# Output projection of an encoder trunk: four of eight feature tiles in the attention chain and four with the norm, the tokens in halves

## The chip, the cores and the metric

The kernel runs on one core of one Trainium2 chip. The metric is the device time of one execution in microseconds (us); a kernel's time is the median of its runs. TensorE (PE) multiplies, VectorE (DVE) and ScalarE (ACT) split, add and evict, GpSimd (POOL) adds a part of the norm's sums, and SyncE (SP) issues most of the loads.

## What is computed

Two requests, 512 and 256 tokens wide, go through the same two layers. Here only what lies around the output projection matters:

```python
def encoder_trunk(x, ...):
    for layer in range(DEPTH):            # DEPTH = 2, D_MODEL = 1024, D_FF = 4096
        if layer % 2 == 0:
            ...                           # windowed and grouped-query attention
            x = x + jnp.concatenate([a_out, b_out], axis=-1) @ w_out_e[j]
        else:
            ...                           # differential attention, norm of each head
            x = x + o.reshape(B, T, DIFF_WIDTH) @ w_out_o[j]
        h = rmsnorm(x, ln_mlp[layer])
        x = x + jnp.square(jax.nn.relu(h @ w_up[layer])) @ w_down[layer]
    return rmsnorm(x, ln_f)
```

## The kernel before

All 768 tokens stand side by side, features on the 128 partitions. `x` has eight tiles of 128 x 768, and so has `o`, the output of attention. A product is made in three matmuls, since every fp32 operand is split into a rounded part (`whi`, `oh`, `xh`) and the rest (`wlo`, `ol`, `xl`): hi by hi, lo by hi, hi by lo. ACT makes the rounded part and DVE the rest.

**Attention and its chain.** An attention unit is one head (or pair of heads) for 128 queries: scores on PE (`gs`, `ns`, `ds`), a softmax on DVE and ACT, a transposition on PE (`npt`, `dpt`), the product with the values (`npv`, `dpv`), and in the odd layer a norm of the head on ACT, DVE and POOL and one more transposition (`otp`). `attention` sets 48 units in a row. While a unit's softmax runs, PE works on the `Chain`: the input projections and, as its last member, `out_proj` (L762 to L774). The chain is pulled a step at a time, and `ramp` (L634, L759) says by a list of marks how many steps stand beside each group of six units. Between the scores of a unit and its transposition stand the chain's steps of that unit and the value product of the unit before.

**The output projection** is in two parts. `out_proj` multiplies the first six tiles of `o` in the chain: for each of the eight feature tiles `m` 18 pairs of matmuls, one of 512 columns (`opa`) and one of 256 (`opb`) with the same weights, a step being the three pairs of one `k`: 48 steps in a layer. `out_proj_norm` (L776 on) follows when the chain is drained. It multiplies the last two tiles of `o` for one half of the tokens (384 columns) at a time, as `opc` (`product`, L788): six matmuls for each `m` and half. After each, DVE adds the result onto `x[m]`, ACT squares it, and POOL or DVE adds the square onto `acc`.

**The norm.** When half 0 is through, `woven` (L817) sets three pieces of half 1 (`m` 0 to 2, 3 to 5, 6 and 7) around the norm of half 0: after the first piece the sums over the partitions (`ss`, L172) and the power (`rt`, on POOL), after the second the spreading of `rt` over the partitions (`pb`, L195) and its copy `R` (L199), and then `split_half`: for each `k` a normed `xn` (L803), its `xh` (L806) and its `xl` (L807). The first matmuls of the up projection (`upc`, L883) take `xh` and `xl` of half 0, and stand right behind the third piece.

**What sets the order.** The order on each engine is made ahead of the run by a scheduler that goes by the order of the code and an estimate of what is ready. In the trace each engine runs its instructions in that order, so one that waits holds up all that is queued behind it. Buffers come from pools: four pairs `whi`/`wlo` of weights, nine `xo` tiles that hold `o` and `x` alike, three PSUM banks "mm" and five "at".

Of the kernel before, what the change touches and what calls it, by code (L numbers as in the profile page):

```python
# [12 lines left out]
F32 = mybir.dt.float32  # L13
F32R = mybir.dt.float32r
AF = mybir.ActivationFunctionType
# [31 lines left out]
def kernel(ctx: ExitStack, tc: tile.TileContext, a: dict, y: bass.AP):  # L47
# [23 lines left out]
    def ps_tile(tag, name):  # L71
        return psum.tile([P, 512], F32, tag=tag, name=name, bufs=BANKS[tag])
# [141 lines left out]
    def proj_feat(lhs, xs, ks, pa, pb, cols=SEGS, nk=None, pin=False):  # L214


        nk = len(ks) if nk is None else nk
        for k in ks:
            xh, xl = xs[k]
            for i, (part, mv) in enumerate(((0, xh), (0, xl), (1, xh))):  # L220
                for ps, (s, e) in ((pa, cols[0]), (pb, cols[1])):
                    if ps is not None:
                        mm = nc.tensor.matmul(ps[:, : e - s], lhs(k, part), mv[:, s:e],  # L223
                                              start=(k == 0 and i == 0), stop=(k == nk - 1 and i == 2))
                        if pin and k == 0 and i == 0:
                            tc.keep_in_program_order(mm)
            yield

    def run(gen):
        for _ in gen:  # L230
# [93 lines left out]
    def even_attention():  # L324
# [306 lines left out]
                       lambda: out_proj("w_out_e", o, lambda m: a["xT"][:, m, :], x)])  # L631
        units = [G(gqa_unit, j, t) for j in range(4) for t in range(TT)]
        units += [G(na_unit, p, t) for p in range(4) for t in range(TT)]
        attention(units, chain, ramp((52, 72, 88, 104, 120, 140, 172, 196, 232)))  # L634
        chain.drain()
        return o, x, es

# [1 line left out]
    def odd_attention(xs, nm, sg, spill):  # L639
# [116 lines left out]
            order += [G(proj_v, h // 2)] * (h % 2 == 0) + [G(proj_qk, h)]  # L756
        chain = Chain(order + [lambda: out_proj("w_out_o", o, lambda m: spill[:, m, :], x)])
        units = [G(diff_unit, h, t) for h in range(8) for t in range(TT)]
        attention(units, chain, ramp((56, 92, 128, 164, 200, 236, 272, 306, 336)))  # L759
        chain.drain()  # L760
        return o, x, es


    def out_proj(src, o, xsrc, x):

        os_ = [split(o[k], "o") for k in range(6)]
        for m in range(KD):
            hi, lo = wtile(src, 6 * P)
            pa, pb = ps_tile("mm", "opa"), ps_tile("mm", "opb")
            yield from proj_feat(lambda k, prt: (hi, lo)[prt][:, k * P : (k + 1) * P], os_, range(6), pa, pb)  # L770
            x[m] = xo_tile("x1")
            nc.sync.dma_start(x[m], xsrc(m))
            xm = x[m]
            evac_halves(pa, pb, lambda ps, s: nc.vector.tensor_tensor(out=xm[:, s], in0=ps, in1=xm[:, s], op=ALU.add))  # L774

    def out_proj_norm(src, o, x, g, mp):  # L776


        os_ = [split(o[k], "o") for k in (6, 7)]
        ws = [wtile(src, 1024) for _ in range(2)]  # L780
        up_ws = [[wtile("w_up", 1024) for _ in range(2)]]
        hs = [htiles(mp) for _ in range(GF)]
        acc = cpool.tile([P, NT], F32, tag="acc", name="acc", bufs=1)
# [1 line left out]
        xs = [None] * KD  # L785
        norms = [Norm(lambda: mp.tile([P, NH], F32, tag="st", name="sq", bufs=3), half, acc) for half in EVEN]

        def product(i, m):  # L788

            sl = slice(*EVEN[i])  # L790
            ps = ps_tile(("mm", "at")[m % 2], "opc")[:, :NH]
            hi, lo = ws[m // 4]
            for k in range(2):
                for j, (part, mv) in enumerate(((0, os_[k][0]), (0, os_[k][1]), (1, os_[k][0]))):
                    c = ((m % 4) * 2 + k) * P
                    last = nc.tensor.matmul(ps, (hi, lo)[part][:, c : c + P], mv[:, sl],
                                            start=(k == 0 and j == 0), stop=(k == 1 and j == 2))
            nc.vector.tensor_tensor(out=x[m][:, sl], in0=ps, in1=x[m][:, sl], op=ALU.add)
            norms[i].add(x[m], KD - 1)
            return last  # L800

        def normed(k, out, s):
# [26 lines left out]
                        split_half(i)  # L829
                last = nm.last  # L830

        products = lambda i, ms: lambda: [product(i, m) for m in ms][-1]
        products(0, range(KD))()
        woven(0, [products(1, ms) for ms in (range(3), range(3, 6), range(6, 8))])

        hold = [cpool.tile([P, NT], F32, tag="acc", name="t4", bufs=1), xo_tile("t4")]
# [414 lines left out]
def _layout(i):  # L1251
# [24 lines left out]

    def out_layout(w):
        w = w.reshape(8, P, KD, P)
        p0 = w[:6].transpose(2, 1, 0, 3).reshape(-1)
        p1 = w[6:].reshape(2, P, 2, 4, P).transpose(2, 1, 3, 0, 4).reshape(-1)  # L1280
        return np.concatenate([p0, p1])

    wx = i["w_out_e"][0]
    d["w_out_e"] = out_layout(np.concatenate([wx[hcols(512, heads)], wx[:512]], 0))
# [59 lines left out]
```

## Time and profile before

| | us |
|---|---|
| median of 3 runs | 1769.04 (1768.12 to 1770.06) |
| the profiled execution | 1770.32 |
| its span, first to last instruction | 1768.6 |
| PE busy in the span | 1731.0 (98%) |
| DVE, ACT, POOL busy | 1253.4, 924.8, 223.8 |
| mean granted TensorE clock | 0.996 of full speed |

The times inside the kernel are counted from the start of the span. A busy PE is not a PE at its peak, since matmuls overlap and their ends are modelled: where two matmuls follow each other, what the second costs is the distance between the two starts. A gap in brackets in the timeline is idle time of the engine just before the row, and behind the arrow stands what ended it.

### The profile page before, as it was taken

To read this page: it belongs to the slowest core of one execution; us is meant where nothing else is said; L and a number is where in the kernel's file an instruction comes from. 1 tells how busy PE (TensorE), PEld (TensorE's weight loads), DVE (VectorE), ACT (ScalarE), POOL (GpSimd) and SP (SyncE) were. 2 spreads that over 40 slices of the span, in tenths; PEclk is the share of its full clock that TensorE was granted. 3 is DMA by queue.
4 is the path that set the end of the run, shared out by engine and by line. 5 is a ranking of instruction groups with operands and counts; after the bars stand their busy time and mean duration, and the time that the engine had idled before them with its cause. 6 is when DMAs were issued, how large, how long until landed. Compare 5 with 4: busy or idle time off the path is not lost.

```text
span 1768.6 us, 28926 instructions
## 1 busy us (share of the span) xinstructions
PE 1731.0 (98%) x11146; PEld 1648.6 (93%) x11146; DVE 1253.4 (71%) x2446; ACT 924.8 (52%) x1933; POOL 223.8 (13%) x302
## 2 busy tenths in 40 slices
PE   7999999999999999999999999999899999999998
PEld 7878888899999999999999999988899999999997
DVE  7878646569566669877566767776696666687775
ACT  6765544345566664552435555554455666645434
POOL 3421000020000000110221212220200000001101
PEclk9999999999999999999999999999999999999999
DMA  5111123312466556653311101122123656466622
GB/s 179 49 34 38 65 82 98 122 36 66 140 183 183 170 182 218 196 128 113 133 49 49 49 25 43 48 61 95 43 66 100 187 183 188 144 245 177 160 83 72
DMA packets 55786, 198.24 MB, mean 112 GB/s; under 512 B 6496, under 2 KB 9312, under 8 KB 50528
## 3 DMA queue, kind: packets, MB, share of 16 engines
q1 hardware_dynamic: 42112, 148.39, 26.0%
q0 software_dynamic: 8064, 14.68, 5.3%
q10 hardware_dynamic: 5472, 33.32, 5.2%
q8 instruction: 88, 1.44, 0.3%
q14 instruction: 50, 0.41, 0.1%
HBM read 158.62 MB, written 36.96 MB: 111 GB/s over the span
## 4 chain that ended last, share of the span: by engine, by line
PE 84%; DVE 7%; DMA 4%; ACT 2%; issue 2%; POOL 1%; POOLq 0%; DVEq 0%; ACTq 0%; SPq 0%
PE upx L949 12%; PE dnx L949 9%; PE dqk L209 8%; PE upz L949 6%; PE dnz L949 4%; PE dvp L209 4%; PE upc L883 4%; PE opa L223 4%; DMA hf<-h 3%; PE upy L949 3%; PE dnb L223 3%; PE dna L223 3%; PE npa L223 2%; PE ds L291 2%; PE dny L949 2%; PE dpv L734 2%
## 5 line engine op out<-in xcount | busy, mean ns | idle before, releaser
L91 DVE TENSOR_TENSOR wlo<-wraw,whi 128x1024 fp32r<-128x1024 f32 (+4 forms) x252 | 235.4, 938 | 144.1 <-ACT whi L90 143.7
L90 ACT ACTIVATE whi<-wraw 128x1024 fp32r<-128x1024 f32 (+4 forms) x248 | 203.4, 825 | 163.4 <-PE dnx L949 79.6
L209 PE MATMUL dqk<-whi,xh 128*128 128x256 f32 x384 | 115.6, 301 | 0.0
L209 PE MATMUL dqk<-whi,xl 128*128 128x256 f32 x384 | 108.6, 283 | 0.0
L209 PE MATMUL dqk<-wlo,xh 128*128 128x256 f32 x384 | 108.4, 282 | 0.0
L719 ACT ACTIVATE de<-ds,m 128x512 f32<-128x512 f32 (+1 forms) x96 | 58.3, 613 | 79.9 <-DVE m L717 79.7
L97 POOL DMA_DIRECT2D wlo<-in_w_up_dram x28 | 24.8, 886 | 452.5 <-DVE hf L969 273.7
L209 PEld LDWEIGHTS dqk<-whi,xh 128*128 128x128 f32 x384 | 73.1, 190 | 8.5 <-issue 7.7
L949 PE MATMUL upx<-xh,whi 128*128 128x384 f32 x224 | 74.8, 334 | 0.0
L949 PE MATMUL upx<-xl,whi 128*128 128x384 f32 x224 | 74.8, 334 | 0.0
L949 PE MATMUL upx<-xh,wlo 128*128 128x384 f32 x224 | 74.8, 334 | 0.0
L949 PE MATMUL upx<-Th,whi 128*128 128x384 f32 x224 | 74.8, 334 | 0.0
L949 PE MATMUL upx<-Tl,whi 128*128 128x384 f32 x224 | 74.8, 334 | 0.0
L949 PE MATMUL upx<-Th,wlo 128*128 128x384 f32 x224 | 74.8, 334 | 0.0
L209 PEld LDWEIGHTS dqk<-wlo,xh 128*128 128x128 f32 x384 | 73.3, 191 | 0.0
L209 PEld LDWEIGHTS dqk<-whi,xl 128*128 128x128 f32 x384 | 73.1, 190 | 0.0
L95 ACT ACTIVATE whi<-wraw 128x512 fp32r<-128x512 f32 x56 | 35.2, 629 | 70.2 <-PE upy L949 36.6
L1063 DVE TENSOR_TENSOR x<-x,dnx 128x384 f32<-128x384 f32 x96 | 52.8, 550 | 22.8 <-PE dnx L949 22.7
L687 DVE SCALAR_TENSOR_TENSOR t<-dqk,rt,ropeO 128x128 f32<-128x128 f32 x192 | 57.6, 343 | 8.1 <-PE dqk L209 8.1
L158 POOL TENSOR_TENSOR acc<-acc,sq 128x384 f32<-128x384 f32 (+2 forms) x24 | 31.2, 1302 | 249.8 <-ACT sq L153 249.0
L90 ACT ACTIVATE whi<-ws 128x1024 fp32r<-128x1024 f32 (+2 forms) x52 | 51.8, 997 | 21.1 <-PE dnz L949 15.1
L97 POOL DMA_DIRECT2D wlo<-in_w_down_dram x28 | 24.6, 879 | 289.9 <-ACT wlo L96 148.4
(347 smaller groups left out, 6092.6 us busy)
## 6 DMA issues: line engine op xcount, KB each, us to landing
wraw<-in_w_up_dram SPq DMA_DIRECT2D x64, 512.0 KB, 3.6
h<-hf ACTq DMA_DIRECT2D x20, 1344.0 KB, 5.2
hf<-h SPq DMA_DIRECT2D x20, 1344.0 KB, 7.2
wraw<-in_w_down_dram SPq DMA_DIRECT2D x52, 512.0 KB, 3.5
wraw<-in_w_in_o_dram SPq DMA_DIRECT2D x24, 512.0 KB, 3.6
wraw<-in_w_in_e_dram SPq DMA_DIRECT2D x16, 512.0 KB, 3.7
wlo<-in_w_up_dram POOLq DMA_DIRECT2D x28, 256.0 KB, 6.1
wlo<-in_w_down_dram POOLq DMA_DIRECT2D x28, 256.0 KB, 4.9
```

Of the source, the lines that this page charges most:

```text
L90: nc.scalar.activation(hi, raw, AF.Copy)
L91: nc.vector.tensor_tensor(out=lo, in0=raw, in1=hi.bitcast(F32), op=ALU.subtract)
L97: nc.gpsimd.dma_start(lo, src, accum_op=ALU.add)
L209: nc.tensor.matmul(ps[:, :256], st[:, tk], col(k, part, 0, 256), start=(k == 0 and i == 0), stop=(k == KD - 1 and i == 2))
L223: mm = nc.tensor.matmul(ps[:, : e - s], lhs(k, part), mv[:, s:e], start=(k == 0 and i == 0), stop=(k == nk - 1 and i == 2))
L291: nc.tensor.matmul(out[h], q(a_, hp, qs), k(b_, hp, ks), start=i == 0, stop=i == 2)
L687: nc.vector.scalar_tensor_tensor(out=tt[:, c].rearrange("p (a d) -> p a d", d=32), in0=ps[:, c].rearrange("p (a d) -> p a d", d=32), scalar=r,
L719: nc.scalar.activation(e, s, AF.Exp, bias=m, scale=1.0, accum_out=l2[:, c : c + 1])
L734: nc.tensor.matmul(pv, pt[:, i * P : (i + 1) * P], v[:, k0 // P + i, vc], start=(i == 0), stop=(i == nk - 1))
L883: last = nc.tensor.matmul(ps, lhs(f0 + f, k, part), mv[:, s:e], start=(n == 0 and j == 0), stop=(n == KD - 1 and j == 2))
L949: mm = nc.tensor.matmul(ps, w[part][:, c], mv, start=(start and kk == 0 and j == 0), stop=(stop and kk == len(form) - 1 and j == 2), skip_ ...
L1063: nc.vector.tensor_tensor(out=xm[:, c], in0=xm[:, c], in1=ps, op=op)
```

## The change

The output projection is cut anew. In the chain, `out_proj` takes the first four tiles of `o` instead of six, and for each `m` it goes through the two halves of the tokens in turn (`proj_half`), 12 matmuls of 384 columns each, all named `opa`, in two steps: 32 steps in a layer instead of 48. `out_proj_norm` takes the other four tiles, 12 matmuls instead of six for each `m` and half. The rounded parts and rests of its last two tiles are made in the pool of the MLP (`Th`, `Tl`) instead of `oh` and `ol`. The first four `m` of half 0 run through `k` 0 and 1 for all four before `k` 2 and 3. The weights of the norm's part need four pairs of buffers instead of two, so that those of the up projection, which are asked for right behind, wait for the output projection's to be done with. The marks of `ramp` follow the shorter chain.

```diff
+    def proj_half(lhs, xs, ps, cols):
+        s, e = cols
+        for k in range(len(xs)):
+            xh, xl = xs[k]
+            for i, (part, mv) in enumerate(((0, xh), (0, xl), (1, xh))):
+                nc.tensor.matmul(ps[:, : e - s], lhs(k, part), mv[:, s:e], ...)
+            if k % 2 == 1:
+                yield
-        attention(units, chain, ramp((52, 72, 88, 104, 120, 140, 172, 196, 232)))
+        attention(units, chain, ramp((52, 72, 88, 104, 120, 142, 172, 193, 216)))
-        attention(units, chain, ramp((56, 92, 128, 164, 200, 236, 272, 306, 336)))
+        attention(units, chain, ramp((56, 91, 128, 163, 200, 236, 270, 297, 320)))
     def out_proj(src, o, xsrc, x):
-        os_ = [split(o[k], "o") for k in range(6)]
+        os_ = [split(o[k], "o") for k in range(KH)]
         for m in range(KD):
-            hi, lo = wtile(src, 6 * P)
-            pa, pb = ps_tile("mm", "opa"), ps_tile("mm", "opb")
-            yield from proj_feat(..., os_, range(6), pa, pb)
+            if m % 2 == 0:
+                w = wtile(src, 1024)
             x[m] = xo_tile("x1")
             nc.sync.dma_start(x[m], xsrc(m))
-            evac_halves(pa, pb, lambda ps, s: nc.vector.tensor_tensor(out=xm[:, s], in0=ps, ...))
+            for s, e in EVEN:
+                ps = ps_tile("mm", "opa")
+                yield from proj_half(..., os_, ps, (s, e))
+                nc.vector.tensor_tensor(out=x[m][:, s:e], in0=ps[:, :NH], in1=x[m][:, s:e], op=ALU.add)
     def out_proj_norm(src, o, x, g, mp):
-        os_ = [split(o[k], "o") for k in (6, 7)]
-        ws = [wtile(src, 1024) for _ in range(2)]
+        os_ = [split(o[k], "o") for k in (4, 5)]
+        for k in (6, 7):
+            os_.append([mp.tile([P, NT], F32R, tag=t, name=t, bufs=6) for t in ("Th", "Tl")])
+            nc.scalar.activation(os_[-1][0], o[k], AF.Copy)
+            nc.vector.tensor_tensor(out=os_[-1][1], in0=o[k], in1=os_[-1][0].bitcast(F32), ...)
+        ws = [wtile(src, 1024) for _ in range(4)]
-        def product(i, m):
-            ps = ps_tile(("mm", "at")[m % 2], "opc")[:, :NH]
-            for k in range(2):
+        def product(i, ms):
+            ps = {m: ps_tile(("mm", "at")[m % 2], "opc")[:, :NH] for m in ms}
+            for ks in ((0, 1), (2, 3)):
+                for m in ms:
+                    for k in ks:
...
-        products(0, range(KD))()
+        product(0, range(4))
+        products(0, range(4, KD))()
         woven(0, [products(1, ms) for ms in (range(3), range(3, 6), range(6, 8))])
```

The layout of the two output weights on the host follows.

The first place is the queue of DVE in the norm stage of the even layer, around the copy `R`. Of the names, `x_...<-opc` is the addition of one `m` of half 1, `wlo<-wraw,whi` the rest of a weight tile of the up projection, `acc<-acc,sq` the norm's sum. Before:

```order
L798 TENSOR_TENSOR x_3997<-opc,x_3997 128x384
L91 TENSOR_TENSOR wlo<-wraw,whi 128x1024
L798 TENSOR_TENSOR x_4081<-opc,x_4081 128x384
L798 TENSOR_TENSOR x_4165<-opc,x_4165 128x384
L199 COPY R<-pb 128x384
L158 TENSOR_TENSOR acc<-acc,sq 128x384
L803 SCALAR_TENSOR_TENSOR xn<-x_3717,gains,R 128x384
L803 SCALAR_TENSOR_TENSOR xn<-x_4081,gains,R 128x384
L803 SCALAR_TENSOR_TENSOR xn<-x_3831,gains,R 128x384
L798 TENSOR_TENSOR x_4249<-opc,x_4249 128x384
L807 TENSOR_TENSOR xl<-xn,xh 128x384 x3
```

The same stretch now:

```order
L817 TENSOR_TENSOR x_3840<-opc,x_3840 128x384
L91 TENSOR_TENSOR wlo<-wraw,whi 128x1024
L817 TENSOR_TENSOR x_3912<-opc,x_3912 128x384
L817 TENSOR_TENSOR x_4005<-opc,x_4005 128x384
L199 COPY R<-pb 128x384
L91 TENSOR_TENSOR wlo<-wraw,whi 128x1024
L158 TENSOR_TENSOR acc<-acc,sq 128x384
L822 SCALAR_TENSOR_TENSOR xn<-x_3635,gains,R 128x384
L822 SCALAR_TENSOR_TENSOR xn<-x_3912,gains,R 128x384
L822 SCALAR_TENSOR_TENSOR xn<-x_3701,gains,R 128x384
L826 TENSOR_TENSOR xl<-xn,xh 128x384 x3
```

A weight tile's rest has come between `R` and the first `xn`, and the addition of `m` 6 has left its place ahead of the first `xl`. The other engine's side of this stretch is short to tell: between `pb` and the first `upc` PE has 24 matmuls `opc` where it had 12, and as many more in each of the pieces ahead.

The second place is the queue of PE at the end of the odd layer's attention, where the last unit's value product `dpv` and the last `otp` stand. Before:

```order
L312 MATMUL otp<-ident,o_tok 128x128
L796 MATMUL opc<-oh,whi 128x384
L796 MATMUL opc<-ol,whi 128x384
L796 MATMUL opc<-oh,wlo 128x384
L796 MATMUL opc<-oh,whi 128x384
L796 MATMUL opc<-ol,whi 128x384
L734 MATMUL dpv<-dv_12401,dpt 128x128 x2
L796 MATMUL opc<-oh,wlo 128x384
L796 MATMUL opc<-oh,whi 128x384
L796 MATMUL opc<-ol,whi 128x384
L796 MATMUL opc<-oh,wlo 128x384
L312 MATMUL otp<-ident,o_tok 128x128
```

The same stretch now:

```order
L323 MATMUL otp<-ident,o_tok 128x128
L814 MATMUL opc<-oh,whi 128x384
L814 MATMUL opc<-ol,whi 128x384
L814 MATMUL opc<-oh,wlo 128x384
L814 MATMUL opc<-oh,whi 128x384
L814 MATMUL opc<-ol,whi 128x384
L814 MATMUL opc<-oh,wlo 128x384
L745 MATMUL dpv<-dv_12389,dpt 128x128 x2
L323 MATMUL otp<-ident,o_tok 128x128
```

The four matmuls that stood between the last `dpv` and the last `otp` stand elsewhere; behind that `otp` twelve `opc` on the tiles 4 and 5 follow, and then the first ones on `Th` and `Tl`.

## Rows read from the trace of the kernel before

**Rows 1.** The page's part 1: busy time, share, instructions.
```profile
PE 1731.0 (98%) x11146; PEld 1648.6 (93%) x11146; DVE 1253.4 (71%) x2446; ACT 924.8 (52%) x1933; POOL 223.8 (13%) x302
```
**Rows 2.** Stretches: length, busy PE, PEld, DVE, ACT, POOL, granted clock, DMA.
```profile
372.70:376.05 3.35, 0.77 (x3) 0.30 (x2) 3.13 (x7) 2.63 (x4) 0.19 (x1) 1.00 0.23 94
...
377.30:380.50 3.20, 3.20 (x12) 3.20 (x11) 3.20 (x8) 2.10 (x5) 0.00 (x0) 0.50 0.02 5
...
1264.10:1267.60 3.50, 0.76 (x3) 0.30 (x2) 3.11 (x7) 2.63 (x4) 0.35 (x1) 1.00 0.23 95
...
1268.40:1271.30 2.90, 2.90 (x10) 2.90 (x10) 2.90 (x7) 1.58 (x3) 0.00 (x0) 0.50 0.00 0
```
**Rows 3.** Timeline of PE, even layer's norm: start, us, engine, line, instruction, idle.
```profile
369.91 0.83 PE L195 MATMUL pb<-ident,rt 128*128 128x128 f32 x6
...
372.51 0.34 PE L796 MATMUL opc<-oh,wlo 128*128 128x384 f32 x1
374.62 0.62 PE L883 MATMUL upc<-xh,whi 128*128 128x384 f32 x2 [1.77 <-ACT xh L806]
376.05 0.44 PE L883 MATMUL upc<-xl,whi 128*128 128x384 f32 x1 [0.81 <-DVE xl L807]
```
**Rows 4.** Timeline of DVE, the same stage, and a weight split earlier.
```profile
352.76 1.22 DVE L91 TENSOR_TENSOR wlo<-wraw,whi 128x1024 fp32r<-128x1024 f32 x1
...
368.94 1.70 DVE L91 TENSOR_TENSOR wlo<-wraw,whi 128x1024 fp32r<-128x1024 f32 x1 [0.36 <-ACT whi L90]
...
371.50 0.54 DVE L199 COPY R<-pb 128x384 f32<-128x384 f32 x1
372.92 0.56 DVE L158 TENSOR_TENSOR acc<-acc,sq 128x384 f32<-128x384 f32 x1 [0.88 <-POOL acc L158]
373.39 1.67 DVE L803 SCALAR_TENSOR_TENSOR xn<-x,gains,R 128x384 f32<-128x384 f32 x3
...
375.45 1.49 DVE L807 TENSOR_TENSOR xl<-xn,xh 128x384 fp32r<-128x384 f32 x3
```
**Rows 5.** Timeline of ACT, then of POOL, in that stage.
```profile
374.04 1.58 ACT L806 ACTIVATE xh<-xn 128x384 fp32r<-128x384 f32 x3 [0.27 <-DVE xn L803]
...
368.53 2.99 POOL L158 TENSOR_TENSOR acc<-acc,sq 128x384 f32<-128x384 f32 x2
```
**Rows 6.** Timeline of PE: two steps of three pairs, and three matmuls of 384.
```profile
287.02 0.40 PE L223 MATMUL opa<-ol,whi 128*128 128x512 f32 x1
...
288.06 0.39 PE L223 MATMUL opa<-ol,whi 128*128 128x512 f32 x1
...
355.23 0.33 PE L796 MATMUL opc<-oh,wlo 128*128 128x384 f32 x1
...
355.75 0.34 PE L796 MATMUL opc<-oh,wlo 128*128 128x384 f32 x1
```
**Rows 7.** Timeline of PE, end of the odd layer's attention, and its first sums.
```profile
1243.00 0.65 PE L734 MATMUL dpv<-dv,dpt 128*128 128x128 f32 x4
1243.41 0.42 PE L796 MATMUL opc<-oh,wlo 128*128 128x384 f32 x1
...
1245.81 0.33 PE L312 MATMUL otp<-ident,o_tok 128*128 128x128 f32 x1 [1.45 <-DVE o_tok L744]
...
1256.72 0.38 PE L172 MATMUL ss<-ones,acc 128*128 128x2 f32 x2 [0.44 <-DVE acc L158]
```
**Rows 8.** Timelines of PE and DVE: one attention unit of the odd layer.
```profile
1157.39 0.50 PE L291 MATMUL ds<-d 64*128 64x512 f32 x2
...
1163.43 0.60 PE L301 MATMUL dpt_ps<-ident,de 128*128 128x128 f32 x4
...
1161.44 0.74 DVE L724 SCALAR_TENSOR_TENSOR de<-de,cf 128x512 f32<-128x512 f32 x1
```
**Rows 9.** DMA issues: KB each, median us from issue to landing.
```profile
x<-in_xT_dram SPq DMA_DIRECT2D x16, 384.0 KB, 5.4
...
x<-spill SPq DMA_DIRECT2D x8, 384.0 KB, 4.2
```

More of the change, by code (lines that the diff above doesn't have):

```diff
@@ L227, in proj_feat @@
             yield
+    def proj_half(lhs, xs, ps, cols):
[3 more added lines that the diff above has]
+            for i, (part, mv) in enumerate(((0, xh), (0, xl), (1, xh))):
+                nc.tensor.matmul(ps[:, : e - s], lhs(k, part), mv[:, s:e],
+                                 start=(k == 0 and i == 0), stop=(k == len(xs) - 1 and i == 2))
+            if k % 2 == 1:
+                yield
     def run(gen):
@@ L764, in out_proj @@
     def out_proj(src, o, xsrc, x):
-        os_ = [split(o[k], "o") for k in range(6)]
+        os_ = [split(o[k], "o") for k in range(KH)]
         for m in range(KD):
-            hi, lo = wtile(src, 6 * P)
-            pa, pb = ps_tile("mm", "opa"), ps_tile("mm", "opb")
-            yield from proj_feat(lambda k, prt: (hi, lo)[prt][:, k * P : (k + 1) * P], os_, range(6), pa, pb)
+            if m % 2 == 0:
+                w = wtile(src, 1024)
             x[m] = xo_tile("x1")
             nc.sync.dma_start(x[m], xsrc(m))
-            xm = x[m]
-            evac_halves(pa, pb, lambda ps, s: nc.vector.tensor_tensor(out=xm[:, s], in0=ps, in1=xm[:, s], op=ALU.add))
+            for s, e in EVEN:
+                ps = ps_tile("mm", "opa")
+                yield from proj_half(lambda k, part: w[part][:, (m % 2 * KH + k) * P : (m % 2 * KH + k + 1) * P], os_, ps, (s, e))
+                nc.vector.tensor_tensor(out=x[m][:, s:e], in0=ps[:, :NH], in1=x[m][:, s:e], op=ALU.add)
     def out_proj_norm(src, o, x, g, mp):
-        os_ = [split(o[k], "o") for k in (6, 7)]
-        ws = [wtile(src, 1024) for _ in range(2)]
+        os_ = [split(o[k], "o") for k in (4, 5)]
+        for k in (6, 7):
+            os_.append([mp.tile([P, NT], F32R, tag=t, name=t, bufs=6) for t in ("Th", "Tl")])
+            nc.scalar.activation(os_[-1][0], o[k], AF.Copy)
+            nc.vector.tensor_tensor(out=os_[-1][1], in0=o[k], in1=os_[-1][0].bitcast(F32), op=ALU.subtract)
+        ws = [wtile(src, 1024) for _ in range(4)]
         up_ws = [[wtile("w_up", 1024) for _ in range(2)]]
@@ L786, in out_proj_norm @@
         norms = [Norm(lambda: mp.tile([P, NH], F32, tag="st", name="sq", bufs=3), half, acc) for half in EVEN]
-        def product(i, m):
+        def product(i, ms):
             sl = slice(*EVEN[i])
-            ps = ps_tile(("mm", "at")[m % 2], "opc")[:, :NH]
-            hi, lo = ws[m // 4]
-            for k in range(2):
[L794 to L799, printed above, removed]
+            ps = {m: ps_tile(("mm", "at")[m % 2], "opc")[:, :NH] for m in ms}
+            for ks in ((0, 1), (2, 3)):
+                for m in ms:
+                    for k in ks:
+                        for j, (part, mv) in enumerate(((0, os_[k][0]), (0, os_[k][1]), (1, os_[k][0]))):
+                            c = ((m % 2) * KH + k) * P
+                            last = nc.tensor.matmul(ps[m], ws[m // 2][part][:, c : c + P], mv[:, sl],
+                                                    start=(k == 0 and j == 0), stop=(k == KH - 1 and j == 2))
+            for m in ms:
+                nc.vector.tensor_tensor(out=x[m][:, sl], in0=ps[m], in1=x[m][:, sl], op=ALU.add)
+                norms[i].add(x[m], KD - 1)
             return last
@@ L830, in woven @@
                 last = nm.last
-        products = lambda i, ms: lambda: [product(i, m) for m in ms][-1]
-        products(0, range(KD))()
+        products = lambda i, ms: lambda: [product(i, [m]) for m in ms][-1]
+        product(0, range(4))
+        products(0, range(4, KD))()
         woven(0, [products(1, ms) for ms in (range(3), range(3, 6), range(6, 8))])
@@ L1278, in out_layout @@
         w = w.reshape(8, P, KD, P)
-        p0 = w[:6].transpose(2, 1, 0, 3).reshape(-1)
-        p1 = w[6:].reshape(2, P, 2, 4, P).transpose(2, 1, 3, 0, 4).reshape(-1)
-        return np.concatenate([p0, p1])
+        return w.reshape(2, KH, P, KD // 2, 2, P).transpose(0, 3, 2, 4, 1, 5).reshape(-1)
     wx = i["w_out_e"][0]
```

## The prediction

> **What bounds the kernel now.** I read the page's busy shares first. PE is busy for 1731.0 us of the span, 98% [rows 1], so no other engine's work counts by itself: a change can gain only where PE stands still, runs at the lower clock, or gets less to do. Next I read stretches with their granted clock, to find where PE loses time near the output projection. Each layer has one such place, the start of the up projection. In the even layer PE is busy for 0.77 of 3.35 us and then runs 3.20 us at a granted clock of 0.50, in the odd layer 0.76 of 3.50 us and then 2.90 us at 0.50 [rows 2]. [...]
>
> The timeline of PE says what it waits for. After `pb` at 369.91 it works off 12 matmuls of half 1, the last from 372.51. Then it waits for the first `xh` until 374.62 and for the first `xl` until 376.05 [rows 3]. The timeline of DVE shows why these are late. `R` is copied from 371.50, an addition to `acc` that waits for POOL ends at 373.48, and only then come three `xn` and, from 375.45, the rests [rows 4]; ACT rounds from 374.04 [rows 5]. So the wait that ends last in this stage is a chain through DVE that begins at `pb`, and PE has too little other work to last through it.
>
> **What the two places cost.** Even layer: of the 3.35 us two matmuls account for 0.35 at the distance of 0.173 us that 384 columns take (0.52 us for three [rows 6]), so 3.0 us are lost; half of the 3.20 us at half clock are 1.6 more. Together 4.6 us. Odd layer: 3.50 - 0.35 + 1.45 = 4.6 us. Both: **9.2 us**, about 0.5% of the time. This is the pool that the change can draw on.
>
> **The change, part by part.**
>
> The matmuls themselves. A layer loses 144 pairs of 512 and 256 columns and gains 288 matmuls of 384. Three pairs take from 287.02 to 288.06, 1.04 us; three matmuls of 384 take from 355.23 to 355.75, six of them 1.04 us [rows 6]. Cost and gain are 0. The splits of `o`, the weights' columns and the columns added on DVE stay the same in number, and lie beside PE.
>
> More cover behind `pb`. PE now has 24 matmuls between `pb` and the first `upc` instead of 12: 4.15 us instead of 2.1. With the 0.6 us of `pb` itself it asks for the first `xh` at `pb` + 4.75. When is that there? DVE's queue now reads: addition of `m` 5, `R`, a weight split, `acc`, three `xn`, three `xl`. The addition and `R` end at about `pb` + 1.3 (0.54 for the copy [rows 4], the same for an addition, 0.2 for the hand-over). The split adds 1.22, `acc` 0.5, the first `xn` 0.57, the rounding on ACT 0.53 (a third of 1.58 [rows 5]): `pb` + 4.2, before PE asks. The first `xl` comes after all three `xn`: 1.3 + 1.2 + 0.5 + 1.6 + 0.5 = `pb` + 5.1, while PE has by then run two matmuls, to `pb` + 5.1. From there three `xn` and three `xl` take 1.67 + 1.49 us [rows 4] for three `k`, and PE needs 3 x 6 x 0.173 = 3.1 us for them: level. I leave 0.3 us of waiting a layer. Too little for the clock to fall, going by the nearest row, where it fell after 3.0 us of standing. Gain 9.2 - 0.6 = **8.6 us**, between 4 and 9.2.
>
> The split that is moved into this chain has its own price. A 128 x 1024 split took 1.22 us while POOL was quiet and 1.70 us while POOL added to `acc` [rows 4, 5]. In the new order POOL has one addition for each 2.1 us of matmuls and adds nothing for `m` 5, so I put this split at 1.22. [...]
>
> The same doubling goes ahead of `ss`. In the odd layer PE waits 0.44 us for `acc` there [rows 7]; a piece of 6.2 us instead of 3.1 covers it. Gain **0.4 us**.
>
> The last `otp` of the odd layer. From the last `dpv` at 1243.00 to its `otp` at 1245.81 run 2.81 us through ACT, DVE, POOL and DVE, and `dpv` itself takes 0.41 [rows 7]. Four matmuls stood in between; now none does, so PE stands 2.4 us instead of about 1.6. The moved matmuls are work that comes later. Cost 4 x 0.173 = **0.7 us**; nothing speaks for less, and if the clock falls there, 1.5 more.
>
> The rests of the tiles 6 and 7. They are now made one behind the other after the last unit, so the first products on tile 7 wait for one split of 128 x 768 more. Twelve matmuls on the tiles 4 and 5 and those on tile 6 stand ahead of them. No row shows the meeting: between 0 and 1.2 a layer (a whole wider split [rows 4]); nearer to 0, **0.2 us** a layer.
>
> The `x` of `m` 7. Its load takes the buffer of `o` 6, free only after that tile's rest is made, and takes 5.4 us (even) or 4.2 us (odd) to land [rows 9]. DVE holds its addition third in the queue behind, and with it the PSUM banks that `m` 4 needs. PE has 30 matmuls, 5.2 us, until then. Behind it wait all further additions on DVE, for which nobody is in a hurry. Cost 0 to 0.7 a layer; I take **0.3 us** in all.
>
> The thinner chain. Beside a unit of the last two groups stand 3.5 to 4.5 steps instead of 4 to 6. A unit of 512 keys needs from `ds` at 1157.39 to the end of `de` at 1162.18, 4.8 us, and its transposition stands at 1163.43, 1.25 us later [rows 8]. Counting PE's new order at the distances above, the time from scores to transposition is 5.0 us or more in all units but two of the odd layer, which have 4.6 and 4.9. Those two may wait. The even layer's units have 256 keys, so less to do, and 4.5 us or more. Cost **0.6 us**, between 0 and 2.5.
>
> Sum: 8.6 + 0.4 - 0.7 - 0.4 - 0.3 - 0.6 = **7.0 us**. The profiled execution took 1770.32 us, of which 1768.6 are the span, and would take 1763.3. It lies 1.3 above the median of the runs; against the median the prediction is 1769.04 - 7.0 = **1762.0 us**.
>
> **The rivals.**
>
> 1. The wait comes back in the new place. If the moved split takes 1.70 us and `acc` waits for POOL for 0.88 us again [rows 4], the first `xh` is at `pb` + 5.6 and the `xl` at `pb` + 6.5. PE then stands for 0.85 and about 1 us, and if the clock falls again 1.5 more go: 3.3 of 4.6 us in each layer. Left are 2.6 + 0.4 - 2.0 = 1.0 us: **1768.0**. For it speaks that the split stands right there in the queue; against it, that POOL's additions now have twice the time.
>
> 2. Slower: PE starves in the last two groups of units. The chain is what fills PE while a softmax runs, and a third of the output projection's steps has left it. There are 24 units in the two layers' last groups. From 0.3 us of waiting in each on, the 7 us are eaten; at 0.5 us they cost 12 us in place of the 0.6 counted: 1762.0 + 11.4 = **1773.4**. For it speaks that spare time was only 1.25 us in the unit shown. Against it: the filler lost from a unit is at most two steps, 2 us, where there were six, and the order counted above leaves no more than two units short.
>
> 3. The seam between chain and norm costs more: the clock falls in the 2.4 us before the last `otp` (1.5 us), and the `x` of `m` 7 lands late in both layers (1.1 more). Gain 4.4: **1764.6**.
>
> **How the numbers follow.** The forecast gets 0.65, rival 1 0.13, rival 2 0.07, rival 3 0.15. A measurement of this kernel can tell about 0.2% from no change, 3.5 us, so faster means under 1765.5: the forecast and rival 3, 0.80. Rival 1 is the same, 0.13, and rival 2 slower, 0.07. The best case is the pool with `ss`, less the certain cost at `otp`: 9.2 + 0.4 - 0.7 = 8.9, 1760.1, with a little for what no row shows 1759.5. Upwards the unknown costs at their upper ends and a part of rival 1 reach 1767.0.
>
> **What would show it.** Right: no gap of more than 0.5 us between the last `opc` and the up projection's second `k`, no stretch at 0.50 there, and a gap of about 2.4 us before the last `otp`. The wait for `acc` ahead of the odd `ss` is gone. Wrong: gaps on `dpt` or `npt` of several tenths in many units (rival 2), a gap on `upc` with a fall of the clock (rival 1), one before `opc` that DVE's addition of `opa` ends (rival 3).

## The result, and the profile after

The changed kernel takes **1756.54 us** in the median of four runs (1754.5 to 1757.02), the kernel before 1769.55 beside it: a ratio of 0.9928, with a 95% interval from 0.9915 to 0.994. That is 13.0 us where 7.0 were forecast. The direction was right, the mechanism at the up projection was right, and the time lies 3 us below the range. In a later series of runs, on another chip than the first experiments below, the same pair gave 0.9936 (0.9924 to 0.9948; 1758.33 against 1768.57): 10.2 us. Both are more than the forecast; how much more depends on the execution, and the traces say where.

Part 1 of the page of the changed kernel, ahead of it its span:

```profile
span 1754.9 us, 28904 instructions
...
PE 1724.9 (98%) x11146; PEld 1656.8 (94%) x11146; DVE 1254.8 (72%) x2442; ACT 922.6 (53%) x1929; POOL 225.8 (13%) x302
```

Against [rows 1] PE has as many instructions and is busy for 6.1 us less. Of that 3.8 lie in the first stage of the two up projections, where the granted clock is 1.00 throughout (0.50 for 3.20 and 2.90 us before), and 1.9 in the even layer's output projection. The other 7.6 us of the span's 13.7 are idle time that is gone.

The stretches that answer to [rows 2], in the changed kernel: from `pb` to the first `upc`, and the first 3.2 us of the up projection, even layer and then odd (length, busy PE, PEld, DVE, ACT, POOL, granted clock, DMA share, GB/s):

```profile
366.15:371.01 4.86, 4.86 (x31) 4.86 (x31) 4.55 (x8) 2.73 (x5) 0.39 (x1) 1.00 0.47 136
371.01:374.20 3.19, 3.19 (x20) 3.10 (x19) 3.19 (x8) 2.73 (x5) 0.00 (x0) 1.00 0.18 72
1251.40:1256.30 4.90, 4.90 (x33) 4.90 (x32) 4.55 (x8) 2.74 (x5) 0.42 (x1) 1.00 0.45 144
1256.30:1259.50 3.20, 3.20 (x20) 3.09 (x19) 3.20 (x8) 2.74 (x5) 0.00 (x0) 1.00 0.16 64
```

PE is busy for the whole of each, and the clock stays at 1.00. The timeline of PE in the even layer (start, duration, idle time in brackets) has no bracket at all where [rows 3] have 1.77 and 0.81:

```profile
366.15 0.83 PE L195 MATMUL pb<-ident,rt 128*128 128x128 f32 x6
...
370.84 0.33 PE L814 MATMUL opc<-Th,wlo 128*128 128x384 f32 x1
371.01 0.52 PE L903 MATMUL upc<-xh,whi 128*128 128x384 f32 x2
371.36 0.38 PE L903 MATMUL upc<-xl,whi 128*128 128x384 f32 x1
```

And the queue of DVE that feeds it, to be read beside [rows 4]:

```profile
367.02 0.56 DVE L199 COPY R<-pb 128x384 f32<-128x384 f32 x1
367.50 1.22 DVE L91 TENSOR_TENSOR wlo<-wraw,whi 128x1024 fp32r<-128x1024 f32 x1
368.63 0.55 DVE L158 TENSOR_TENSOR acc<-acc,sq 128x384 f32<-128x384 f32 x1
369.10 1.67 DVE L822 SCALAR_TENSOR_TENSOR xn<-x,gains,R 128x384 f32<-128x384 f32 x3
370.69 1.49 DVE L826 TENSOR_TENSOR xl<-xn,xh 128x384 fp32r<-128x384 f32 x3
```

DVE has no idle time there: the addition to `acc` that waited 0.88 us for POOL before finds it done. The first of the three `xl` is ready about 0.5 us after 370.69 (a third of 1.49), and PE asks for it at 371.36: it fits with some 0.2 us to spare.

**Where the time went, stage by stage.** The stages are cut at PE's first matmul of a name; each number is the time from one to the next, the first one from PE's first matmul at all and the last one to its last.

| stage | before | after | difference |
|---|---|---|---|
| up to the first `opa` | 277.93 | 278.06 | +0.13 |
| first `opa` to first `upc`, even | 91.05 | 87.35 | -3.70 |
| first `upc` to first `upx`, even | 71.39 | 68.69 | -2.70 |
| to the first `ds` of the odd layer | 463.49 | 462.88 | -0.61 |
| first `ds` to first `upc`, odd | 356.69 | 353.71 | -2.98 |
| first `upc` to first `upx`, odd | 71.37 | 68.69 | -2.68 |
| to the end | 424.81 | 423.52 | -1.29 |

The two stages that hold nothing but MLP and what follows (-0.61 and -1.29, 1.9 us together) have no instruction of the change in them. The others give 11.9 us. Summing in these the distance from each matmul's start to the next one's, by name, splits them: standing and half clock at `upc` -9.4; the sums `ss` and the wait ahead of them -1.1; the wait ahead of the last `otp` +0.7; the matmuls of the output projection outside those places -0.5 in the even layer and -1.7 in the odd, of which 0.9 is one stand of before (shown with the second experiment); the attention's own matmuls -0.7 in the even layer (eight `npv` now lie ahead of the first `opa`, whose stage has hardly grown) and +0.9 in the odd.

### The profile page after: what moved, and what is told of

Same layout as the page of the kernel before. It is cut to its first block, busy times and chain, and to the rows that moved or that the text cites. A ratio compares the mean times of both kernels' runs of the same rounds, so it can differ in the third digit from the quotient of the medians.

```text
span 1754.9 us, 28904 instructions
## 1 busy us (share of the span) xinstructions
PE 1724.9 (98%) x11146; PEld 1656.8 (94%) x11146; DVE 1254.8 (72%) x2442; ACT 922.6 (53%) x1929; POOL 225.8 (13%) x302
## 4 chain that ended last, share of the span: by engine, by line
PE 91%; DVE 4%; ACT 2%; issue 1%; DMA 1%; POOL 0%; POOLq 0%; DVEq 0%; ACTq 0%
PE upx L969 13%; PE dnx L969 9%; PE dqk L209 8%; PE upz L969 6%; PE dna L223 5%; PE dnb L223 5%; PE dnz L969 4%; PE dvp L209 4%; PE opa L235 4%; PE opc L814 4%; PE upc L903 4%; PE upy L969 3%; PE npa L223 2%; PE ds L302 2%; PE dny L969 2%; PE dpv L745 2%
```

## The experiments

All are timed beside the kernel before, whose median is 1767.6 us beside the first four and 1768.57 beside the others, on another chip. What they share with it runs 1 to 4 us longer or shorter from one execution to the next (last section), so the verdicts rest on the stages that an edit touches. Where the changed kernel was profiled again these agree to 0.1 us, but for a fall of the clock in the odd layer that comes in one execution and not in the other; of the kernel before one execution was profiled. For the changed kernel the two attention-to-up stages are 87.35 and 353.71 us, for before 91.05 and 356.69.

**The halves alone** (six and two tiles as before):

```diff
+    def proj_half(...)                     # as in the change
...
-            pa, pb = ps_tile("mm", "opa"), ps_tile("mm", "opb")
-            yield from proj_feat(..., os_, range(6), pa, pb)
+            for s, e in EVEN:
+                ps = ps_tile("mm", "opa")
+                yield from proj_half(..., os_, ps, (s, e))
+                nc.vector.tensor_tensor(out=x[m][:, s:e], in0=ps[:, :NH], in1=x[m][:, s:e], op=ALU.add)
```

> The kernel before with one part of the change alone: six tiles stay in the chain and two with the norm, but the chain's 288 pairs of 512 and 256 columns become 576 matmuls of 384, the halves of the tokens in turn. It tells apart where the gain beyond the seam with the norm comes from. Theory A, the shape: outside the hand-overs a pair took 350.9 ns on the mean in the trace of before (234.0 + 117) and two matmuls of 384 took 347.9 in the trace of after; over 288 pairs that is 0.9 to 1.1 us, and up to 1.4 more where single matmuls of a pair stood longer beside the units of the odd layer: 1767 to 1768.6 against 1769.5. The stand and the half clock behind pb stay, about 9.4 us in both layers. Theory B, the prediction's own term (shape worth nothing, the gain beyond the seam is the moving of tiles out of the chain): 1769.5, and the sum over opa equals that over opa and opb to within 0.3 us. Theory C, the shape and not the cover makes the whole gain: 1757 to 1760, with no stand before upc.

Measured: 1765.48 us, a ratio to before of 0.9996 (0.9986 to 1.0006). The chain's matmuls take 51.71 us instead of 52.25 in the even layer and 53.40 instead of 54.04 in the odd, 1.2 us in all, about what theory A had for them (0.9 to 1.1). But the odd stage does not get shorter by it (356.91 instead of 356.69): `dqkT` takes 0.7 and the last `otp` 0.2 more, at other meetings with the units. The stand before `upc` is all there:

```profile
376.64 0.62 PE L894 MATMUL upc<-xh,whi 128*128 128x384 f32 x2 [1.76 <-ACT xh L817]
378.07 0.55 PE L894 MATMUL upc<-xl,whi 128*128 128x384 f32 x1 [0.82 <-DVE xl L818]
```

So the new shape by itself gives nothing that stands out of the noise (the medians lie 2.1 us apart, but the interval of the ratio holds 1), theory C is out, and the gain at `upc` does not come from the shape.

**The moved tiles alone** (four and four, but pairs in the chain):

```diff
-            for s, e in EVEN:
-                ps = ps_tile("mm", "opa")
-                yield from proj_half(..., os_, ps, (s, e))
-                nc.vector.tensor_tensor(out=x[m][:, s:e], in0=ps[:, :NH], in1=x[m][:, s:e], op=ALU.add)
+            pa, pb = ps_tile("mm", "opa"), ps_tile("mm", "opb")
+            yield from proj_feat(..., os_, range(KH), pa, pb)
+            evac_halves(pa, pb, lambda ps, s: nc.vector.tensor_tensor(out=xm[:, s], in0=ps, in1=xm[:, s], op=ALU.add))
```

> The changed kernel with the other part undone: four tiles in the chain and four with the norm, but the chain works with pairs of 512 and 256 columns as before (192 pairs). Theory A: the seam stays as in the changed kernel, no stand before upc, no stretch at half clock; 192 pairs at 3 to 3.7 ns more than two matmuls of 384 cost 0.6 to 0.7 us, single longer matmuls beside the units up to 1 more: 1757.1 to 1758.2. Theory B: within 0.3 us of the changed kernel, 1756.5. Theory C: most of the gain is gone, 1763 or more.

Measured: 1759.71 us, 0.9954 (0.9942 to 0.9966). `upc` starts without a stand and its stage takes 68.69 us in both layers, as in the changed kernel. The other stages are longer than the changed kernel's, 88.54 against 87.35 and 355.89 against 353.71. In them the chain's matmuls take 1.1 and 1.0 us more, of which the steady 3 to 3.7 ns a pair explain 0.3 to 0.36 each. Another 0.3 in each layer sits on three pairs between whose matmuls a unit comes. In the kernel before, an `opb` behind a unit took 0.36 us (at 1177.92), one right behind its `opa` 0.28 (at 1175.06). The rest was not taken apart. In the odd stage 1.1 us more lie in and behind the stand ahead of the last `otp`, where the clock fell to 0.50 (below). That is theory A in kind. In size it is above A's 1.6 to 1.7 us: 1.2 in the even stage and 2.2 in the odd, 2.1 together without the fall. With the tiles moved the halves are worth about 1 us a layer, which they were not alone.

What a torn pair looks like, in the timeline of PE of the kernel before:

```profile
1175.89 0.27 PE L312 MATMUL otp<-ident,o_tok 128*128 128x128 f32 x1
1175.91 0.48 PE L223 MATMUL opa<-oh,whi 128*128 128x512 f32 x1
1177.01 1.16 PE L734 MATMUL dpv<-dv,dpt 128*128 128x128 f32 x8 [0.61 <-DVE dpt L305]
1177.92 0.36 PE L223 MATMUL opb<-oh,whi 128*128 128x256 f32 x1
```

`opa` stands alone between two matmuls of the attention, PE then waits 0.61 us for `dpt`, and `opb` follows behind eight `dpv`. From 1175.91 to 1177.01 are 1.10 us for a matmul that takes 0.23 elsewhere. No such stand is left in the changed kernel; but there is none either with the moved tiles alone or with the halves alone, so it is not shown which part of the change it takes.

**Five and three tiles:**

```diff
-        os_ = [split(o[k], "o") for k in range(KH)]
+        os_ = [split(o[k], "o") for k in range(5)]
...                                          # weights of five tiles for each m
-        os_ = [split(o[k], "o") for k in (4, 5)]
+        os_ = [split(o[5], "o")]
...
-        ws = [wtile(src, 1024) for _ in range(4)]
+        ws = [wtile(src, 1024) for _ in range(3)]
...                                          # product(): k 0, then k 1 and 2
```

> The middle: five tiles in the chain, three with the norm, halves in the chain, otherwise as the changed kernel. Behind pb stand 18 matmuls, 3.1 us, instead of 12 or 24, so PE asks for the first xh at pb + 3.7. The moved weight split is not in the queue of VectorE there in this order, the addition to acc is. Theory A (cover against the chain through VectorE): if that addition waits for GpSimd as before, the first xh comes at pb + 4.7 and the first xl at pb + 5.5: 1.0 and 0.4 us of standing in each layer, 2.8 in all, 1759.3; if it doesn't wait, 0 to 0.4 in a layer, 1756.5 to 1757.5. The granted clock stays at 1.00 behind stands this short; if it falls all the same, 1.6 more in each layer, 1762.5. Theory B (the gain goes by the tiles moved, half of it for half of them): 1763.

Measured: 1760.35 us, 0.9961 (0.9947 to 0.9975). PE in the even layer, and the stretch behind:

```profile
371.55 0.61 PE L902 MATMUL upc<-xh,whi 128*128 128x384 f32 x2 [0.20 <-ACT xh L824]
372.52 0.44 PE L902 MATMUL upc<-xl,whi 128*128 128x384 f32 x1 [0.36 <-DVE xl L825]
```
```profile
372.40:375.60 3.20, 3.08 (x18) 3.08 (x18) 3.20 (x8) 1.98 (x6) 0.00 (x0) 1.00 0.00 0
```

18 matmuls behind `pb` leave 1.4 us a layer (by the distances 0.37 at the first `xh` and 1.07 in the up projection's stage, 69.76 against 68.69), and the clock does not fall. The loss at `upc` is 4.7 us a layer with 12 matmuls, 1.4 with 18 and none with 24: not in proportion to the tiles, as theory B had it, since the clock's part goes with the first tile (a granted clock of 0.50 with 12, 1.00 with 18). The addition to `acc` waits only 0.26 us here, and for that case theory A had 0 to 0.4 a layer. The 1.4 are its figure for the other case, made in another way (an `x` addition stands among the first `xl`): that the size agrees is luck. The odd stage has, besides, a fall of the clock to 0.50 behind the last `otp`, which the expectation did not count.

**Useless work as cover:** 12 matmuls more behind `pb` in the kernel before, whose result nobody reads.

```diff
+        def fill(m):
+            ps = ps_tile("at", "fill")[:, :NH]
+            for j in range(6):
+                c = ((m % 4) * 2 + j // 3) * P
+                nc.tensor.matmul(ps, ws[m // 4][j % 3 // 2][:, c : c + P], os_[j // 3][j % 3 % 2][:, NH:NT], ...)
         def product(i, m):
+            if i == 1 and m > 5:
+                fill(m)
```

> The kernel before with nothing but 12 more matmuls of 384 columns between pb and the first upc of each layer, six ahead of the product of m 6 and six ahead of that of m 7, into a bank that nobody reads: 24 x 0.1735 = 4.2 us of work that is of no use. Theory A, cover is what counts: PE asks for the first xh at pb + 4.75, when it is there (pb + 4.7 in the trace of before), stands at most 0.5 us for the first xl, and the clock does not fall. Each layer pays 2.1 us and gets back about 2.5 of the standing and 1.6 of the half clock: 2.0 a layer, 1765.5, faster with more work. If the clock falls all the same: about 0.4 a layer, 1768.7. Theory B, the wait goes along with the work, or comes from the order on VectorE: slower by the work, 1773.7.

Measured: 1764.39 us against 1767.6, 0.9982 (0.9972 to 0.9992): **faster with 4.2 us more work**. PE and DVE in the even layer, and the stretch that ran at 0.50 before:

```profile
370.21 0.83 PE L195 MATMUL pb<-ident,rt 128*128 128x128 f32 x6
...
375.07 0.34 PE L892 MATMUL upc<-xh,whi 128*128 128x384 f32 x1
375.85 0.45 PE L892 MATMUL upc<-xl,whi 128*128 128x384 f32 x1 [0.44 <-DVE xl L816]
```
```profile
373.17 0.56 DVE L158 TENSOR_TENSOR acc<-acc,sq 128x384 f32<-128x384 f32 x1 [0.88 <-POOL acc L158]
373.65 1.67 DVE L812 SCALAR_TENSOR_TENSOR xn<-x,gains,R 128x384 f32<-128x384 f32 x3
375.24 1.49 DVE L816 TENSOR_TENSOR xl<-xn,xh 128x384 fp32r<-128x384 f32 x3
```
```profile
377.00:380.00 3.00, 3.00 (x19) 3.00 (x19) 3.00 (x7) 1.58 (x3) 0.00 (x0) 1.00 0.02 5
```

The chain through DVE is the old one up to the three `xn`, with its wait of 0.88 us for POOL; only PE has something to do meanwhile. Behind the `xn` one thing is new: the product of `m` 6 now ends later, so its addition no longer stands ahead of the first `xl`, which brings them 0.5 us earlier in each layer. The stand shrinks to 0.6 (odd layer: 0.8), and the clock stays at 1.00 behind it in both layers. From the first `opa` to the first `upx` the even layer takes 160.62 us instead of 162.44, and from the first `ds` to the first `upx` the odd 426.19 instead of 428.06: 1.8 and 1.9 us less, where theory A said 2.0 a layer. This isolates the cause: with the shape and the chain to the first `xh` as they were, cover brings back 8.0 of the 9.4 us at `upc`, of which at most 0.9 go through the addition that moved. The 1.4 that are left are the waits for `xl`, and they are gone in the changed kernel, where the addition to `acc` finds POOL done.

**The changed kernel once more**, for what comes again:

> The changed kernel once more, beside the kernel before on the chip of the four kernels above, where before has a median of 1767.6. Theory A, most of what the two profiled executions differ by comes from the change: from the first opa to the first upc 87.35 us again (91.05 before), from the first ds to the first upc of the odd layer 353.71 (356.69 before), the first upc's stage 68.69, each to 0.1 us; only the MLP and the stage ahead of the first opa vary, by 1 to 2 us. 1756.0 to 1757.5, a ratio to before near 0.994. If the clock falls behind the last otp, where PE stands for 2.3 us, the odd stage is 1.2 to 1.6 longer, as in the kernels with pairs and with five tiles. Theory B, the 6 us beyond the forecast are chance: 1759.5 to 1760.5, a ratio of 0.996, with stages that come out differently this time.

Measured: 1758.33 us, 0.9936 (0.9924 to 0.9948). The even stage is 87.36 us, the up projections 68.69 and 68.70: the same. The odd stage is 355.05 instead of 353.71. Two stretches of this execution, the stand before the last `otp` and what follows:

```profile
1221.30:1223.50 2.20, 0.08 (x1) 0.00 (x0) 0.74 (x3) 0.77 (x3) 0.55 (x1) 1.00 0.45 88
1224.60:1227.70 3.10, 3.10 (x11) 3.10 (x11) 1.83 (x2) 1.13 (x2) 0.00 (x0) 0.50 0.26 41
```

The same two stretches of the first execution:

```profile
1219.40:1221.56 2.16, 0.00 (x1) 0.00 (x1) 0.67 (x3) 0.77 (x3) 0.55 (x1) 1.00 0.42 83
1222.50:1225.50 3.00, 3.00 (x18) 2.74 (x17) 1.83 (x2) 1.26 (x2) 0.00 (x0) 1.00 0.20 27
```

The stand is 2.2 us in both; the clock falls to 0.50 behind one and not behind the other, which is 1.3 us. Theory A holds for the stages, with the fall that it named; the median of 1758.33 lies 0.8 above its range. This execution is itself the longest of its six, by the fall and by 3.8 us in the stage ahead of the first `opa` (last section).

**Each `m` through all four `k` in turn**, the new order of half 0 undone:

```diff
-        product(0, range(4))
-        products(0, range(4, KD))()
+        products(0, range(KD))()
```

> The changed kernel without the new order of half 0: each m runs through all four k before the next, instead of k 0 and 1 for four m ahead of k 2 and 3. PE then asks for the rests of the tiles 6 and 7 some 12 to 18 matmuls (2 to 3 us) earlier. Theory A, these rests are on the path and the order is what hides them: PE stands 1 to 2.5 us more behind the last otp or npv in each layer, 1758.5 to 1761. Theory B, the matmuls on the tiles 4 and 5 that the banks allow hide them in either order: within 0.5 us of the changed kernel.

Measured: 1758.91 us, 0.9945 (0.9932 to 0.9958). Stages 87.34 and 355.13, with the same fall of the clock behind the last `otp` as in the execution above (matmuls of 384 columns 0.32 us apart instead of 0.17): no difference beyond 0.1 us. Theory B; the rests of the tiles 6 and 7 are hidden in either order.

**A thinner end of the chain:**

```diff
-        ... ramp((52, 72, 88, 104, 120, 142, 172, 193, 216))
+        ... ramp((52, 72, 88, 104, 120, 142, 172, 199, 216))
-        ... ramp((56, 91, 128, 163, 200, 236, 270, 297, 320))
+        ... ramp((56, 91, 128, 163, 200, 236, 270, 303, 320))
```

> The changed kernel with a thinner end of the chain: in the last group of six units 17 steps instead of 23 in both layers, the six steps moved into the group before. The prediction's third rival said that PE starves beside these units. Counted from the new order of PE, scores and transposition of the odd layer's last six units lie 4.6, 5.0, 5.0, 5.5, 3.4 and 3.9 us apart instead of 5.9, 6.5, 5.6, 6.0, 5.0 and 6.0 (as counted, 384 columns at 0.1735 us); a unit of 512 keys needs about 4.8 us from the scores to the end of de, one of 256 keys less. Theory A, the chain of the changed kernel has steps to spare: 0.4 to 1.5 us slower than the changed kernel, from stands ahead of dpt of the odd layer, 1757 to 1758. Theory B, it is at its edge: each of the twelve units of the two groups stands 0.5 us more, 6 us, 1762.5.

Measured: 1758.19 us, 0.9944 (0.993 to 0.9958). (The expectation calls the rival the third; in the prediction it is the second.) The odd stage takes 355.51 us, again with a fall of the clock (0.32 us between matmuls behind the last `otp`): 0.5 more than the 355.05 of the changed kernel with one. In the even layer the first `opa` comes earlier by the moved steps, so the stages are not comparable; from the first `ns` to the first `upc` it takes 180.53 us, the changed kernel 180.43. The only wait of PE in the units of the odd layer's last three groups that the trace puts down is this (engine, line, what for, total, times, longest):

```profile
PE opa L235 <- DVE ol L129: 0.4, 1, 0.4
```

It is not one for a softmax. With a quarter fewer steps in the last group nothing starves, so the changed kernel's own chain has steps to spare: theory A, at its lower end and not by the stands ahead of `dpt` that it named.

**Three steps held back** for the last unit of the odd layer: one ahead of the last `dpv`, two between it and the last `otp`.

```diff
         live[0][3]()
-        live[1][2]()
+        if targets[-1] % 4:
+            chain.pull(targets[-1] + 1)
+        last = live[1][2]()
+        if last is not None:
+            with tc.issue_after(last.ins):
+                chain.drain()
         live[1][3]()
...
-        attention(units, chain, ramp((56, 91, 128, 163, 200, 236, 270, 297, 320)))
+        attention(units, chain, ramp((56, 91, 128, 163, 200, 236, 270, 297, 317)))
```

> The changed kernel with the last three steps of the odd layer's chain held back: one stands ahead of the last dpv, two (12 matmuls, 2.1 us) between it and the last otp. Nothing else is changed. Theory A, the stand of 2.3 us before that otp is paid for by nothing else: it shrinks to 0.2 to 0.4 us, and the clock cannot fall behind it; 2 us less than the changed kernel, up to 3.5 against an execution in which the clock falls: 1754 to 1755. Theory B, it comes back ahead of the last dpt or dpv, or as waits for the rests of tile 7 behind the otp: no change against the changed kernel.

Measured: 1756.8 us against 1758.33 of the changed kernel beside it, 0.9931 of before (0.9919 to 0.9943). The intervals overlap, and the time lies above the 1754 to 1755 that were expected, but the stage is clear: 351.79 us instead of 353.71 or 355.05. The timeline of PE:

```profile
1219.46 0.61 PE L750 MATMUL dpv<-dv,dpt 128*128 128x128 f32 x4
...
1221.82 0.34 PE L235 MATMUL opa<-oh,wlo 128*128 128x384 f32 x1
1222.23 0.33 PE L328 MATMUL otp<-ident,o_tok 128*128 128x128 f32 x1
```

Twelve matmuls fill the stand, 0.2 us of it is left, and the clock does not fall: behind the `otp` matmuls of 384 columns follow each other at 0.17 us, where they were 0.32 us apart in the second execution of the changed kernel. 1.9 to 3.3 us less in the stage, by cover at the place from which the change had taken it: theory A for the stage. It has the shortest odd stage of all versions, but its time does not set it apart. The profiled execution lost as much elsewhere: its even layer's MLP, which has the same instructions in the same order on PE, DVE and ACT, runs 3.4 us longer than in the first execution of the changed kernel, with these waits:

```profile
PE dnx L975 <- DVE x L1089: 3.9, 3, 1.9
```

## Why the prediction was right in the mechanism and too small in the size

**The bound and the pool: right.** The two stands with their half clock were counted at 9.2 us; their places gave 9.4.

**More cover behind `pb`: right, 0.8 us too cautious.** The prediction put the first `xh` at `pb` + 4.2 and the first `xl` at `pb` + 5.1. The trace has the last of three `xn` and ACT's rounding run from 369.10, so `xh` about 4.1 and `xl` about 5.0 us behind 366.15, and PE comes at 4.86 and 5.21. The 0.3 us of waiting that were left in each layer did not come.

**The moved split: at its lower end, as taken.** It took 1.22 us in both layers. In each POOL is busy for 0.4 of the 4.9 us around it, and done before it starts. In the kernel with useless matmuls a split of this size took 1.66 us where it started while POOL was adding, as the 1.70 of [rows 4] did. In the changed kernel another split, ahead of `R`, meets an addition that starts after it: the split takes 1.23 us, and it is POOL that takes 1.58 instead of 1.01:

```profile
363.11 1.23 DVE L91 TENSOR_TENSOR wlo<-wraw,whi 128x1024 fp32r<-128x1024 f32 x1 [0.36 <-ACT whi L90]
363.63 1.58 POOL L158 TENSOR_TENSOR acc<-acc,sq 128x384 f32<-128x384 f32 x1 [1.54 <-ACT sq L153]
365.53 1.01 POOL L158 TENSOR_TENSOR acc<-acc,sq 128x384 f32<-128x384 f32 x1 [0.32 <-ACT sq L153]
```

**`ss`: right place, mis-sized.** 0.4 was counted from the one bracket in [rows 7]. By the distances 0.6 went with that wait, 0.15 ahead of the even layer's `ss`, and 0.4 within the `ss` matmuls of both layers: 1.1. (Each of the two pieces ahead of `pb` has 36 matmuls instead of 18, so 18 more and not 12 as between `pb` and `upc`.)

**The last `otp`: right.** 0.7 us more standing, as counted (2.32 against 1.61, by the distances). The fall of the clock behind it, the first half of rival 3, is what usually happens: of the six profiled executions with this stand of 2.0 to 2.3 us five have it, for 1.3 us where 1.5 was named, and the first of the changed kernel has not. So the forecast case had the less likely outcome at this place.

**The step that failed** is the group of small terms for the chain and its matmuls. The prediction gave the matmuls themselves 0 and charged 1.3 us for rests, `x` of `m` 7 and a thinner chain. The traces give a gain of about 2.0 us there (0.5 + 1.7 + 0.7 - 0.9). Three terms were wrong:

- *Matmuls: 0.* Three pairs in 1.04 us [rows 6] is the best case, read from one spot. Over all pairs outside the hand-overs between units and chain a pair took 351 ns and two matmuls of 384 347 to 348: 0.4 to 0.5 us a layer; the first experiment has 0.54 and 0.64. Pairs lose more at hand-overs, where a unit can come between the two (0.3 us a layer on three pairs); the second experiment has about 1 us a layer for pairs against halves.
- *Rests of tiles 6 and 7, `x` of `m` 7: 0.7.* From the first `opa` to the end of the up projection's first stage no matmul of the output projection but those behind the last `dpv` waits 0.3 us in either layer of after. The order that was thought to hide the rests is not even needed.
- *Thinner chain: 0.6, and up to 12 in rival 2.* No wait on a softmax; even with a last group a quarter thinner the loss is 0.5. The two units that were counted at 4.6 and 4.9 us and might wait did not.

**What was not the change.** The sum set 7.0 against a trace of before in which the MLP happened to run long. The waits of PE in the even layer's MLP (engine, line, what for, total, times, longest), before:

```profile
PE dnx L949 <- DVE x L1063: 3.1, 3, 1.3
```

and in the kernel with useless matmuls, whose DVE has the same order from there on:

```profile
PE dnx L958 <- DVE x L1072: 1.3, 2, 0.7
PE dnx L958 <- ACT whi L90: 0.9, 1, 0.9
```

Its two MLP stages take 0.8 and 0.7 us less than before's, without an edit there, and the changed kernel with three steps held back has 3.9 us of such waits, though the order on PE, DVE and ACT in the even layer's MLP is the same in all these kernels. So most of the 1.9 us that the stage table shows for the MLP is one execution against another. Against the forecast's 7.0 then stand 11.9 us of the first pair of traces, or 10.6 with the fall of the clock, which is close to the 10.2 of the second measurement: a miss of 3.6 to 4.9 us, of which about 3.3 lie in the group of small terms, 0.8 at the seam and 0.7 at `ss`.

**The rivals.** Rival 1 (the wait comes back) and rival 2 (PE starves) did not occur; the first half of rival 3 did in most executions, its second half, a late `x` of `m` 7, in none. Rival 1's own numbers give 0.5 us for the stand at `xl`, not about 1, which makes it 1767.2 and not 1768.0. The range's lower end, 1759.5, was the pool with `ss`, less the `otp`, and 0.6 for what no row shows. It was too high because all small terms were given a loss or zero, though a changed meeting of chain and units can as well gain.

What stays open: the +0.9 us in the attention's own matmuls of the odd layer (0.7 of it on `dqk`) comes in all kernels with the new marks and was not taken apart, nor was the 0.7 that the even layer gains on its units.

## What to carry to other kernels

Cover was worth more here than the stand that it filled, since the clock fell to 0.50 behind the stand: 4.2 us of useless matmuls made this kernel 3.2 us faster in the median. Where work can be moved, put it behind the point where the longest chain through the other engines begins, and look what it leaves uncovered where it came from: three steps held back for that place made its stage 1.9 us shorter, though the whole time does not show it clearly. In a sum of small terms give each both signs, take a duration as the mean over all its rows and not from the best spot, and check the baseline's own trace for waits that another execution doesn't have.

## What the runs showed of the hardware that was not expected

The clock's fall after a stand is not a matter of the stand alone here. It fell to 0.50 behind 2.2 us of standing in one execution of the changed kernel and not in another (rows above), and behind the 1.45 us of [rows 7] it did not (1.00). With 1.98 us of idle time ahead of that `otp` it fell to 0.50 in the kernel with pairs; behind the 0.4 to 0.8 us of standing at `upc`, in the kernels with five tiles and with useless work, it stayed at 1.00. What else decides it, no run here shows.

The clock also differs where the kernels are equal. Two stretches of the early attention, in the kernel before and in the changed kernel's second execution:

```profile
100.00:120.00 20.00, 17.97 (x137) 15.54 (x137) 16.27 (x32) 12.51 (x34) 4.04 (x4) 1.00 0.13 37
120.00:140.00 20.00, 17.86 (x132) 14.73 (x132) 14.64 (x27) 13.51 (x34) 4.08 (x4) 1.00 0.12 32
```
```profile
100.00:120.00 20.00, 18.95 (x137) 16.79 (x136) 15.14 (x31) 11.24 (x31) 4.03 (x4) 0.91 0.13 37
120.00:140.00 20.00, 18.29 (x115) 15.45 (x115) 13.10 (x24) 11.24 (x29) 3.97 (x4) 0.83 0.07 14
```

The granted clock is 1.00 and 1.00 in one, 0.91 and 0.83 in the other, and the stage from the first `qp` to the first `opa` takes 248.6 and 252.5 us. This part of the program, which the change leaves alone up to these stretches, moves the whole time by up to 4 us, a third of the gain. It does not go with the change: the kernel with the halves alone shows the same 0.91 and 0.83, the first execution of the changed kernel 1.00 and 1.00. A difference of 2 us between versions has to be read from the stages.
